# RMSNorm on one core: rows scaled on ScalarE, multiplied by gamma in bulk on VectorE, the rest in two passes on GpSimd

**Chip, cores, metric.** One core of a Trainium2 chip. The metric is device time in microseconds (us) of a whole execution, as the median of several; the profile's span is of one execution and is 1.7 to 2.5 us shorter.

## The reference

```python
x: (16, 1024, 512) float32, gamma: (512,) float32
rms = np.sqrt(np.mean(x ** 2, axis=-1, keepdims=True) + 1e-5)
return (x / rms * gamma).astype(np.float32)
```

33.6 MB are read and 33.6 MB written. The work is 4 tiles of 128 partitions x 32 rows x 512 columns, 8.39 MB each.

## The kernel before

Two kinds of on-chip memory appear below, SBUF and PSUM; in this kernel PSUM holds gamma's copy from TensorE and squares that wait to be summed. Three SBUF slots hold a tile each; tile 3 takes slot 0 after tile 0 has been stored. One row needs a sum of squares (ScalarE, for half of the groups with VectorE), a root (ScalarE), a reciprocal and one fused multiply (VectorE).

```python
load(0, 0, 0, 8); load(0, 0, 8, 32)          # SyncE's queue; (tile, slot, first row, last row)
nc.scalar.dma_start(out=gamma_row, in_=gamma.unsqueeze(0))
# ... ones x gamma_row in TensorE -> PSUM -> gamma_b [128, 512] in SBUF, copied by VectorE

def apply(slot, g, rstd):                    # 8 rows
    for r in range(G):
        nc.vector.scalar_tensor_tensor(
            out=slots[slot][:, g + r, :], in0=slots[slot][:, g + r, :],
            scalar=rstd[:, r : r + 1], in1=gamma_b, op0=OP.mult, op1=OP.mult)

def transfers(t, g):                         # after the rows of (t, g) are done
    if (t, g) == (0, 0):
        store(0, 0, 0, 1); load(1, 1, 0, 32); load(2, 2, 0, 16)
        store(0, 0, 1, 2); load(2, 2, 16, 32)
    elif (t, g) == (0, 24):
        store(0, 0, 2, 16); store(0, 0, 16, 32); load(3, 0, 0, 16); load(3, 0, 16, 32)
    elif (t, g) == (1, 24): store(1, 1, 0, 32)
    elif (t, g) == (2, 24): store(2, 2, 0, 32)
    elif (t, g) == (3, 8):  store(3, 0, 0, 16)
    elif (t, g) == (3, 24): store(3, 0, 16, 32)

ahead = row_stats(0, 0)
for k, (t, g) in enumerate(groups):          # the sums run one group ahead; a scheduler orders the rest
    ...
```

## Time and profile before

| | before |
|---|---|
| time, median (range) of 4 | 162.13 us (161.92 to 162.3) |
| span of the profiled run | 160.4 us |
| busy: VectorE, ScalarE, GpSimd | 122.6, 80.1, 0.2 us |
| share of the bulk transfer queue | 97.7% |
| tile 1, 2, 3a, 3b: store issued at | 85.6, 115.8, 131.1, 146.3 us |

The store times read as dates: in this kernel each store is issued before the queue ahead of it is empty, and the transfers run without a hole (422 to 436 GB/s from 2 to 157.6 us). The prediction shows the lines, and calls the times at which the queue would run empty the times at which it "wants" a tile. Below, "3a" and "3b" are tile 3's halves.

### The profile page before, as it was taken

Reading aid. Unit: us, or ns where it says so; the run is one execution under the profiler, and the core shown is the slowest. Engines: PE = TensorE matmul, PEld = TensorE weight load, DVE = VectorE, ACT = ScalarE, POOL = GpSimd, SP = SyncE. Lnnn points to the kernel's source line nnn. Section 1 sums busy time; section 2 is a strip of 40 time slices with the busy share of each in tenths; the row PEclk is TensorE's granted clock in tenths of the full one; section 3 lists DMA queues with packets and bytes.
Section 4 is the critical chain, followed back from the end, with each engine's and each line's share of the span. In section 5 each row is a group of like instructions: output and inputs, shape, how many; then the busy total and the mean of one; then the engine's idle time right before and its main releaser. Section 6 shows DMA issues by size and latency. Waiting matters only on the chain.

```text
span 160.4 us, 410 instructions
## 1 busy us (share of the span) xinstructions
PE 2.0 (1%) x2; PEld 0.5 (0%) x2; DVE 122.6 (76%) x163; ACT 80.1 (50%) x162; POOL 0.2 (0%) x4
## 2 busy tenths in 40 slices
PE   4000000000000000000000000000000000000000
PEld 1000000000000000000000000000000000000000
DVE  0100928999999519999999999999999999994000
ACT  3098039990390999996900950079609940000000
POOL 0000000000000000000000000000000000000000
DMA  5999999699699999999999999998998998999993
GB/s 197 523 392 392 466 449 523 261 523 523 262 402 387 455 458 418 453 415 466 409 392 498 409 400 507 409 507 376 425 507 360 441 507 360 417 400 441 449 417 147
DMA packets 2164, 67.13 MB, mean 419 GB/s; under 512 B 241, under 2 KB 241, under 8 KB 498
## 3 DMA queue, kind: packets, MB, share of 16 engines
q1 hardware_dynamic: 2160, 67.11, 97.7%
q14 instruction: 2, 0.02, 0.0%
q10 hardware_dynamic: 2, 0.00, 0.0%
HBM read 33.56 MB, written 33.55 MB: 418 GB/s over the span
## 4 chain that ended last, share of the span: by engine, by line
DVE 67%; DMA 13%; ACT 7%; issue 2%; DVEq 0%; SPq 0%
DVE slot L88 48%; DVE ss L71 18%; DMA slot<-in_x_dram 13%; ACT sq_scratch L76 3%; ACT sq L70 3%; DVE rstd L83 1%; DVEq L154 0%; ACT rms L82 0%; SPq L42 0%
## 5 line engine op out<-in xcount | busy, mean ns | idle before, releaser
L88 DVE SCALAR_TENSOR_TENSOR slot<-slot,rstd,gamma_b 128x512 f32<-128x512 f32 x128 | 85.8, 738 | 0.1
L76 ACT ACTIVATE sq_scratch<-slot 128x512 f32<-128x512 f32 x64 | 40.0, 625 | 10.0 <-DMA slot<-in_x_dram 8.7
L70 ACT ACTIVATE sq<-slot 128x2048 f32<-128x2048 f32 x16 | 29.8, 1864 | 18.6 <-DVE ss L71 11.5
L71 DVE TENSOR_REDUCE ss<-sq 128x4 f32<-128x2048 f32 x16 | 35.9, 2274 | 3.4 <-ACT sq L70 3.4
L82 ACT ACTIVATE rms<-ss,eps_t 128x8 f32<-128x8 f32 x16 | 4.6, 297 | 25.9 <-DVE ss L71 25.7
L83 DVE RECIPROCAL rstd<-rms 128x8 f32<-128x8 f32 x16 | 3.1, 193 | 16.1 <-ACT rms L82 16.1
L76 ACT ACTIVATION_READ_ACCUMULATOR sq_scratch<-slot 128x1 f32 x64 | 11.9, 186 | 0.0
L57 DVE COPY gamma_b<-sq 128x512 f32<-128x512 f32 x1 | 0.7, 691 | 3.3 <-PE sq L55 3.3
L55 PE MATMUL sq<-gamma_row,ones_col 1*128 1x512 f32 x2 | 2.0, 1122 | 2.2 <-DMA gamma_row<-in_gamma_dram 2.2
L76 ACT ACT_TABLE_LOAD x1 | 1.3, 1283 | 1.3 <-PEq L143 1.3
L82 ACT ACT_TABLE_LOAD x1 | 1.3, 1283 | 0.0
L53 DVE MEMSET ones_col<- 1x128 f32 x1 | 0.2, 165 | 0.8 <-PEq L143 0.8
L55 PEld LDWEIGHTS sq<-gamma_row,ones_col 1*128 1x128 f32 x2 | 0.5, 306 | 2.2 <-issue 2.2
L143 POOL MEMSET const-bfloat16-1.0<- 128x1 bf16 x1 | 0.1, 101 | 0.0
L143 POOL MEMSET const-uint8-127<- 128x1 uint8 x1 | 0.1, 101 | 0.0
L143 POOL MEMSET const-float32-0.0<- 128x1 f32 x1 | 0.1, 98 | 0.2 <-issue 0.2
L143 POOL MEMSET const-float32-1.0<- 128x1 f32 x1 | 0.1, 98 | 0.0
L60 DVE MEMSET eps_t<- 128x1 f32 x1 | 0.1, 59 | 0.0
## 6 DMA issues: line engine op xcount, KB each, us to landing
slot<-in_x_dram SPq DMA_DIRECT2D x4, 4096.0 KB, 27.6
out_dram<-slot SPq DMA_DIRECT2D x3, 4096.0 KB, 18.8
slot<-in_x_dram SPq DMA_DIRECT2D x1, 6144.0 KB, 21.5
out_dram<-slot SPq DMA_DIRECT2D x1, 3584.0 KB
slot<-in_x_dram SPq DMA_DIRECT2D x1, 2048.0 KB, 7.2
out_dram<-slot SPq DMA_DIRECT2D x2, 256.0 KB, 21.3
out_dram<-slot SPq DMA_DIRECT2D x2, 29.8
gamma_row<-in_gamma_dram ACTq DMA_DIRECT2D x1, 2.0 KB
```

The costliest lines, as they stand in the source:

```text
L53: nc.vector.memset(ones_col, 1.0)
L55: nc.tensor.matmul(gamma_psum[:, 0], ones_col, gamma_row, start=True, stop=True)
L57: nc.vector.tensor_copy(out=gamma_b, in_=gamma_psum[:, 0])
L60: nc.vector.memset(eps_t, eps)
L70: nc.scalar.activation(out=sq, in_=slots[slot][:, g + h : g + h + H, :], func=AF.Square)
L71: nc.vector.tensor_reduce(out=ss[:, h : h + H], in_=sq, axis=mybir.AxisListType.X, op=OP.add)
L76: nc.scalar.activation(out=sq_scratch, in_=slots[slot][:, g + r, :], func=AF.Square, accum_out=ss[:, r : r + 1],)
L82: nc.scalar.activation(out=rms, in_=ss, func=AF.Sqrt, bias=eps_t, scale=1.0 / D)
L83: nc.vector.reciprocal(out=rstd, in_=rms)
L88: nc.vector.scalar_tensor_tensor(out=slots[slot][:, g + r, :], in0=slots[slot][:, g + r, :], scalar=rstd[:, r : r + 1], in1=gamma_b, op0=O ...
L143: nc = _bacc.Bacc("TRN2", target_bir_lowering=False, num_devices=1)
```

## The change

The intent is to spread the elementwise work over three engines. ScalarE squares whole groups of rows and scales some rows by the reciprocal; VectorE sums the squares and multiplies those rows by gamma in bulk (one instruction for several rows); GpSimd takes the last rows of a group (its "share", 3 to 8 of 8 or 16) and multiplies them twice. The order on the engines is now written by hand. Cut to the core:

```diff
+    ctx.enter_context(tc.manual_schedule())
+    nc.scalar.addr_align(128, offset=0, max_nops=0)
-    nc.scalar.dma_start(out=gamma_row, in_=gamma.unsqueeze(0))
+    pieces = (0, 96, 176, 256, 336, 416, D)
+    for c0, c1 in zip(pieces, pieces[1:]):
+        nc.scalar.dma_start(out=gamma_row[:, c0:c1], in_=gamma.unsqueeze(0)[:, c0:c1])
-    nc.vector.tensor_copy(out=gamma_b, in_=gamma_psum[:, 0])
+    nc.scalar.copy(out=gamma_b[:, 0], in_=gamma_psum[:, 0])
+    groups = [    # tile, first row, rows, pieces of the squares, GpSimd's share
+        (0, 0, 8, (4, 4), 3), (0, 8, 8, (4, 4), 3), (0, 16, 16, (7, 5, 4), 7),
+        (1, 0, 16, (7, 5, 4), 8), (1, 16, 16, (7, 5, 4), 8), (2, 0, 16, (7, 5, 4), 8),
+        (2, 16, 16, (7, 5, 4), 7), (3, 0, 16, (7, 5, 4), 7), (3, 16, 16, (7, 5, 4), 3)]
+    def scale_by_pool(rstd, t, g, n, share):
+        part = slots[slot_of[t]][:, g + n - share : g + n, :]
+        by_row = rstd[:, n - share : n].to_broadcast([P, share, D])
+        nc.gpsimd.tensor_tensor(out=part, in0=part, in1=by_row, op=OP.mult)
+        last = nc.gpsimd.tensor_tensor(
+            out=part, in0=part, in1=gamma_b.to_broadcast([P, share, D]), op=OP.mult)
+    def scale_rows(rstd, t, g, r0, r1):
+        for r in range(r0, r1):
+            nc.scalar.activation(out=x[:, g + r, :], in_=x[:, g + r, :], func=AF.Copy, scale=rstd[:, r])
+        part = x[:, g + r0 : g + r1, :]
+        nc.vector.tensor_tensor(out=part, in0=part, in1=gamma_b.to_broadcast([P, r1 - r0, D]), op=OP.mult)
     # (0, 0): three single-row stores between the loads of tile 2, instead of two
# ... cut: tile 0 in three loads, load 1 issued at once; tile 2 in three loads; scheduling notes; the loop, whose order on VectorE is, per group of 16:
#     sum 7 rows, sum 5 rows, multiply (first half), sum 4 rows, multiply (second half), reciprocal
```

More of the change, by code (lines that the diff above doesn't have):

```diff
@@ L27 @@
     R = 32
-    G = 8
-    H = 4
     assert N == 4 * P * R
@@ L33 @@
     ov = of.rearrange("(t p r) d -> t p r d", p=P, r=R)
+    ctx.enter_context(tc.manual_schedule())
+    nc.scalar.addr_align(128, offset=0, max_nops=0)
     const = ctx.enter_context(tc.tile_pool(name="const", bufs=1))
-    stats = ctx.enter_context(tc.tile_pool(name="stats", bufs=4))
-    psum = ctx.enter_context(tc.tile_pool(name="psum", bufs=2, space=bass.MemoryType.PSUM))
+    stats = ctx.enter_context(tc.tile_pool(name="stats", bufs=9))
+    psum = ctx.enter_context(tc.tile_pool(name="psum", bufs=1, space=bass.MemoryType.PSUM))
@@ L39 @@
     slots = [const.tile([P, R, D], fp32, name=f"slot{i}") for i in range(3)]
+    before_scale = []
     def load(t, slot, r0, r1):
-        nc.sync.dma_start(out=slots[slot][:, r0:r1], in_=xv[t][:, r0:r1])
+        dma = nc.sync.dma_start(out=slots[slot][:, r0:r1], in_=xv[t][:, r0:r1])
+        before_scale.append((slot, r0, r1, dma))
     def store(t, slot, r0, r1):
-        nc.sync.dma_start(out=ov[t][:, r0:r1], in_=slots[slot][:, r0:r1])
+        dma = nc.sync.dma_start(out=ov[t][:, r0:r1], in_=slots[slot][:, r0:r1])
+        before_scale.append((slot, r0, r1, dma))
@@ L47 @@
     load(0, 0, 0, 8)
-    load(0, 0, 8, 32)
+    load(0, 0, 8, 16)
+    load(0, 0, 16, 32)
+    load(1, 1, 0, 32)
     gamma_row = const.tile([1, D], fp32)
-    nc.scalar.dma_start(out=gamma_row, in_=gamma.unsqueeze(0))
+    pieces = (0, 96, 176, 256, 336, 416, D)
+    for c0, c1 in zip(pieces, pieces[1:]):
+        nc.scalar.dma_start(out=gamma_row[:, c0:c1], in_=gamma.unsqueeze(0)[:, c0:c1])
     ones_col = const.tile([1, P], fp32)
-    nc.vector.memset(ones_col, 1.0)
-    gamma_psum = psum.tile([P, H, D], fp32, name="sq")
+    nc.gpsimd.memset(ones_col, 1.0)
@@ L55 @@
+    gamma_psum = psum.tile([P, 7, D], fp32, name="sq_psum")
     nc.tensor.matmul(gamma_psum[:, 0], ones_col, gamma_row, start=True, stop=True)
-    gamma_b = const.tile([P, D], fp32)
-    nc.vector.tensor_copy(out=gamma_b, in_=gamma_psum[:, 0])
+    gamma_b = const.tile([P, 1, D], fp32)
+    nc.scalar.copy(out=gamma_b[:, 0], in_=gamma_psum[:, 0])
     eps_t = const.tile([P, 1], fp32)
-    nc.vector.memset(eps_t, eps)
-    sq_scratch = const.tile([P, D], fp32)
-    def row_stats(slot, g):
-        ss = stats.tile([P, G], fp32, name="ss")
-        rms = stats.tile([P, G], fp32, name="rms")
-        rstd = stats.tile([P, G], fp32, name="rstd")
-        if (g // G) % 2:
-            for h in range(0, G, H):
-                sq = psum.tile([P, H, D], fp32, name="sq")
-                nc.scalar.activation(out=sq, in_=slots[slot][:, g + h : g + h + H, :], func=AF.Square)
-                nc.vector.tensor_reduce(
-                    out=ss[:, h : h + H], in_=sq, axis=mybir.AxisListType.X, op=OP.add
-                )
-        else:
-            for r in range(G):
-                nc.scalar.activation(
-                    out=sq_scratch,
-                    in_=slots[slot][:, g + r, :],
-                    func=AF.Square,
-                    accum_out=ss[:, r : r + 1],
-                )
-        nc.scalar.activation(out=rms, in_=ss, func=AF.Sqrt, bias=eps_t, scale=1.0 / D)
-        nc.vector.reciprocal(out=rstd, in_=rms)
-        return rstd
@@ L86, in apply @@
-    def apply(slot, g, rstd):
-        for r in range(G):
-            nc.vector.scalar_tensor_tensor(
-                out=slots[slot][:, g + r, :],
-                in0=slots[slot][:, g + r, :],
-                scalar=rstd[:, r : r + 1],
-                in1=gamma_b,
-                op0=OP.mult,
-                op1=OP.mult,
-            )
-    groups = [(t, g) for t in range(4) for g in range(0, R, G)]
-    slot_of = [0, 1, 2, 0]
+    nc.gpsimd.memset(eps_t, eps)
+    groups = [
+        (0, 0, 8, (4, 4), 3),
+        (0, 8, 8, (4, 4), 3),
+        (0, 16, 16, (7, 5, 4), 7),
+        (1, 0, 16, (7, 5, 4), 8),
+        (1, 16, 16, (7, 5, 4), 8),
+        (2, 0, 16, (7, 5, 4), 8),
+        (2, 16, 16, (7, 5, 4), 7),
+        (3, 0, 16, (7, 5, 4), 7),
+        (3, 16, 16, (7, 5, 4), 3),
+    ]
@@ new lines, with square_sums, inverse_rms @@
+    slot_of = [0, 1, 2, 0]
+    def square_sums(ss, t, g, r, m, k):
+        home, name, most = ((psum, "sq_psum", 7), (const, "sq_sbuf", 5))[k % 2]
+        sq = home.tile([P, most, D], fp32, name=name)
+        rows = slots[slot_of[t]][:, g + r : g + r + m, :]
+        nc.scalar.activation(out=sq[:, :m], in_=rows, func=AF.Square)
+        nc.vector.tensor_reduce(
+            out=ss[:, r : r + m, 0], in_=sq[:, :m], axis=mybir.AxisListType.X, op=OP.add
+        )
+    def inverse_rms(ss, n):
+        nc.scalar.activation(out=ss[:, :n, 0], in_=ss[:, :n, 0], func=AF.Sqrt, bias=eps_t, scale=1.0 / D)
+        nc.vector.reciprocal(out=ss[:, :n, 0], in_=ss[:, :n, 0])
+        return ss
@@ new lines, in scale_by_pool @@
+    def scale_by_pool(rstd, t, g, n, share):
[3 more added lines that the diff above has]
+        last = nc.gpsimd.tensor_tensor(
+            out=part, in0=part, in1=gamma_b.to_broadcast([P, share, D]), op=OP.mult
+        )
+        before_scale.append((slot_of[t], g + n - share, g + n, last))
+    def scale_rows(rstd, t, g, r0, r1):
+        x = slots[slot_of[t]]
+        for r in range(r0, r1):
+            nc.scalar.activation(out=x[:, g + r, :], in_=x[:, g + r, :], func=AF.Copy, scale=rstd[:, r])
+        part = x[:, g + r0 : g + r1, :]
+        scaled = nc.vector.tensor_tensor(out=part, in0=part, in1=gamma_b.to_broadcast([P, r1 - r0, D]), op=OP.mult)
+        for slot, b0, b1, earlier in before_scale:
+            if slot == slot_of[t] and b0 < g + r1 and g + r0 < b1:
+                tc.declare_no_dep(scaled.ins, earlier.ins, reason="ScalarE waited for it before it scaled these rows")
@@ L102, in transfers @@
             store(0, 0, 0, 1)
-            load(1, 1, 0, 32)
             load(2, 2, 0, 16)
             store(0, 0, 1, 2)
-            load(2, 2, 16, 32)
-        elif (t, g) == (0, 24):
-            store(0, 0, 2, 16)
+            load(2, 2, 16, 24)
+            store(0, 0, 2, 3)
+            load(2, 2, 24, 32)
+        elif (t, g) == (0, 16):
+            store(0, 0, 3, 16)
             store(0, 0, 16, 32)
@@ L111, in transfers, with pieces_of @@
             load(3, 0, 16, 32)
-        elif (t, g) == (1, 24):
+        elif (t, g) == (1, 16):
             store(1, 1, 0, 32)
-        elif (t, g) == (2, 24):
+        elif (t, g) == (2, 16):
             store(2, 2, 0, 32)
-        elif (t, g) == (3, 8):
+        elif (t, g) == (3, 0):
             store(3, 0, 0, 16)
-        elif (t, g) == (3, 24):
+        elif (t, g) == (3, 16):
             store(3, 0, 16, 32)
-    ahead = row_stats(0, 0)
-    for k, (t, g) in enumerate(groups):
-        rstd = ahead
-        if k + 1 < len(groups):
-            tn, gn = groups[k + 1]
-            ahead = row_stats(slot_of[tn], gn)
-        apply(slot_of[t], g, rstd)
+    def pieces_of(group):
+        t, g, n, pieces, share = group
+        ss = stats.tile([P, 16, 1], fp32, name="ss")
+        r = 0
+        todo = []
+        for k, m in enumerate(pieces):
+            todo.append((ss, t, g, r, m, k))
+            r += m
+        return ss, todo
+    ss, todo = pieces_of(groups[0])
+    for piece in todo:
+        square_sums(*piece)
+    rstd = inverse_rms(ss, groups[0][2])
+    for k, group in enumerate(groups):
+        t, g, n, pieces, share = group
+        mine = n - share
+        half = (mine + 1) // 2
+        ahead = groups[k + 1 :][:1]
+        ss, todo = pieces_of(ahead[0]) if ahead else (None, [])
+        scale_by_pool(rstd, t, g, n, share)
+        for piece in todo[:2]:
+            square_sums(*piece)
+        if n < 16:
+            scale_rows(rstd, t, g, 0, mine)
+        else:
+            scale_rows(rstd, t, g, 0, half)
+        for piece in todo[2:]:
+            square_sums(*piece)
+        if n == 16:
+            scale_rows(rstd, t, g, half, mine)
         transfers(t, g)
+        for nxt in ahead:
+            rstd = inverse_rms(ss, nxt[2])
 _INS = ['x', 'gamma']
```

## The prediction

It is printed as recorded, less passages that are cut and marked. The reason given against the transfer-bound rival and the one given for the lock were of that kind too. Its sums came to: VectorE about 112 us in all; tile 1 ready at 96 us, tile 2 at 130, tile 3's halves at 146 and 152.5, and so the central case of 174 us; under the lock in full 22.6 us a group with 8 GpSimd rows and 20.9 with 7, and so 195 to 201 us. "Port" and "lock" are words for a supposition that no trace had shown. The rival's 1.8 ns a column is an estimate: 58.5 us, from tile 1's first reciprocal near 60 us to 118.5 us, for 31 rows of 512 columns, twice.

> **What bounds the kernel now.** I read the page's slices and queue shares first, then the rates in stretches of the span, then the order of the stores, then the groups.
>
> ```profile
> span 160.4 us, 410 instructions
> ...
> PE 2.0 (1%) x2; PEld 0.5 (0%) x2; DVE 122.6 (76%) x163; ACT 80.1 (50%) x162; POOL 0.2 (0%) x4
> ...
> DMA  5999999699699999999999999998998998999993
> ...
> q1 hardware_dynamic: 2160, 67.11, 97.7%
> ```
>
> No compute engine is full; the queue of bulk transfers is, at 97.7% of the span. The rate in stretches (last two columns: DMA share, GB/s):
>
> ```profile
> 2.00:20.00 18.00, 2.04 (x2) 0.50 (x2) 5.03 (x9) 7.92 (x19) 0.00 (x0) 1.00 0.99 422
> 20.00:60.00 40.00, 0.00 (x0) 0.00 (x0) 31.19 (x37) 26.88 (x46) 0.00 (x0) 1.00 1.00 424
> 60.00:100.00 40.00, 0.00 (x0) 0.00 (x0) 40.00 (x58) 24.92 (x57) 0.00 (x0) 1.00 1.01 436
> 100.00:140.00 40.00, 0.00 (x0) 0.00 (x0) 39.96 (x52) 19.63 (x41) 0.00 (x0) 1.00 1.00 432
> 140.00:157.60 17.60, 0.00 (x0) 0.00 (x0) 6.23 (x10) 0.00 (x0) 0.00 (x0) 1.00 1.00 434
> 157.60:160.40 2.80, 0.00 (x0) 0.00 (x0) 0.00 (x0) 0.00 (x0) 0.00 (x0) 1.00 0.06 23
> ```
>
> From 2 to 157.6 us the transfers run at 422 to 436 GB/s with no hole. The page's chain of work that ended last is 67% VectorE, but that chain only leads back from the last store's issue; what counts is whether a store is issued before the queue in front of it runs dry. SyncE's issues answer that:
>
> ```profile
> 36.95 13.21 SPq L45 DMA_DIRECT2D out_dram<-slot  x2
> 72.22 10.13 SPq L42 DMA_DIRECT2D slot<-in_x_dram  x2
> ...
> 115.83 30.76 SPq L45 DMA_DIRECT2D out_dram<-slot  x3
> ```
>
> At 0.432 MB/us a half tile (16 rows, 4.19 MB) takes 9.7 us, a whole tile 19.4. Stream order: loads 0, 1, 2 with a few rows stored (from 1.7 to about 62 us), rest of tile 0 out (to 80), tile 3 in (to 99), tile 1 out (to 118.5), tile 2 out (to 138), tile 3 out (to 157.5). So the queue wants tile 1 by 99, tile 2 by 118.5, tile 3's halves by 138 and 148. The kernel before issues these at 85.6, 115.8, 131.1 and 146.3 us: margins of 13, 3, 7 and 1.5 us. It's at the transfers' floor, and computing faster buys nothing: without startup and tail the bytes need about 155.5 of the 160.4 us.
>
> ```profile
> L88 DVE SCALAR_TENSOR_TENSOR slot<-slot,rstd,gamma_b 128x512 f32<-128x512 f32 x128 | 85.8, 738 | 0.1
> L70 ACT ACTIVATE sq<-slot 128x2048 f32<-128x2048 f32 x16 | 29.8, 1864 | 18.6 <-DVE ss L71 11.5
> L71 DVE TENSOR_REDUCE ss<-sq 128x4 f32<-128x2048 f32 x16 | 35.9, 2274 | 3.4 <-ACT sq L70 3.4
> ```
>
> These give the unit prices for the new work: squares of 4 rows 1.86 us on ScalarE, their sum 2.27 us (2.2 from start to start) on VectorE.
>
> [...]
>
> **The change part by part.** The bytes are the same, and so is the stream order in all that matters. Splits of loads, a third single-row store (0.26 MB) and gamma in six pieces only shift issues; at 0.51 us an issue on ScalarE, gamma's six end near 4 us, before tile 0's first data (7.98 us). I give them 0 ± 0.5 us. The chains in engine order:
>
> - VectorE loses 85.8 us of row multiplies. It sums the squares of all 128 rows per partition (twice the 35.9 us for 64 rows, less some fixed cost: about 69) and multiplies 74 rows by gamma in bulk[...]. With reciprocals about 112 us, only 11 below 122.6.
> - ScalarE squares all rows in large pieces (about 58 us) and scales 74 rows at an estimated 0.61 us (the 512-column form is 0.625 in the trace with an accumulator): 45. With roots about 106, up from 80.
> - GpSimd gets the other 54 rows (shares 3, 3, 7, 8, 8, 8, 7, 7, 3), twice[...], and cannot start before the first reciprocals.
>
> Per 16-row group: ScalarE 7.2 + 8.5 x 0.61 + 0.3 = 12.7; VectorE 8.9 + 4.6 + 0.2 = 13.7, or about 14.5 with its wait for the first squares[...]. The transfers want a group every 19.4 us of load and store, which looks like enough, but not from where GpSimd starts.
>
> Tile 1 lands near 42 (ScalarE was released by it at 42.74 before). Its first squares (7 rows, 3.1) end near 46; VectorE then sums 3.85 and 2.75, multiplies 2.7, sums 2.2, multiplies 2.2, takes the reciprocal 0.2: near 60. From there GpSimd is back to back[...]. Store 2 starts near 131.4 after issue and first-byte time, a hole of about 13 us. After that 16.8 MB remain: 131.4 + 38.8 = 170.2, and both halves of tile 3 are ready in time (wanted by 150.8 and 160.5). Plus 2.4 us tail gives a span of 172.6; the time is 1.8 above the span before, so about 174 us. That is my central case: the last but one store waits for GpSimd.
>
> **The rivals.**
> - Still bound by transfers. If GpSimd's pass costs at most about 1.8 ns a column and the port isn't taken for whole instructions, tile 2 is ready by about 119 and the hole goes: 161 to 163 us. For it: the shares look fitted to the engine (few rows at both ends, 7 or 8 between), and ScalarE and VectorE alone meet every date.[...]
> - The port lock in full. A 16-row group then runs pass, multiply, pass, multiply in turn[...]. From 62 us (the reciprocal also waits for the lock): tile 1 at 108, tile 2 at 152, holes of about 9 and 24 us plus a few at the end: about 195 to 201 us.[...] Against: a kernel fitted on a chip would not have ended up with this. If blocking is partial, 175 to 190.
> - A gain. The mean rate from 2 to 157.6 us is 430 GB/s and the best stretch 436: running all of it at 436 would save 155.6 x (1 - 430/436) = 2.1 us, 1.3%. Over 2% would need 3.2 us; startup and tail are unchanged.
>
> **Range and chances.** I give the transfer-bound rival 0.36, GpSimd alone 0.25, blocking in part or in full 0.37, a gain 0.02. The number on record is the central case, 174, which also has about half of the weight on either side; the low end must hold the transfer-bound case (161), the high end most of the lock (200). The distribution has two humps, so the number between is the least bad and the range is wide.
>
> **What would show it.** Right: GpSimd[...] back to back from near 60 us; the DMA line falls below 9 around 118 to 131; SyncE's wait for GpSimd ends the wait before tile 2's store. Lock: bulk multiplies on VectorE of 4 to 5 rows showing far over their 2.2 to 2.8 us, or idle time before them with the passes next to them stretched, and holes before tiles 1 and 2. Transfer-bound: the DMA line stays at 9 to the end and store 2 is issued by 118. Wrong in kind: a hole before load 2 or load 3[...].

Some of its prices stand there without a source; the runs give them. VectorE's multiplies by gamma, put at 2.2 us for 4 rows, 2.7 for 5 and 4.6 for a group with 8 GpSimd rows, take 2.28, 2.81 and 2 x 2.28 = 4.56 us in run 1. A sum takes 2.28 us for 2048 columns and 3.89 for 3584 there, so 1.05 ns a column and some 0.13 us fixed. From readiness to a store's first bytes the prediction allows 1.4 us; the first bytes follow the start of an issue by 1.0 us in the kernel before (0.73 to 1.7 us) and by 0.8 us at tile 1's store in the changed one (112.49 to 113.3).

## The result, and the profile after

The changed kernel takes 205.94 us (205.41 to 209.05, 4 runs, one of them slow) against 162.13: a ratio of 1.2692, 95% interval 1.2644 to 1.274. Ratios here are the mean time of one kernel's runs over that of the other's of the same rounds, so not quite the ratio of the medians. That is outside the predicted range, which ended at 200. Executions over 1.5% slower than the fastest of the same kernel are left out of the means. The page of the changed kernel:

```profile
span 203.2 us, 288 instructions
...
PE 2.0 (1%) x2; PEld 0.5 (0%) x2; DVE 156.8 (77%) x50; ACT 108.2 (53%) x111; POOL 108.2 (53%) x24
...
DMA  7999999989999999999500999900004999499297
```

VectorE was to fall to about 112 us and shows 156.8. The transfers, full before, now stand still twice. In stretches (GB/s last):

```profile
2.00:99.00 97.00, 2.04 (x2) 0.49 (x2) 72.14 (x27) 60.83 (x58) 51.09 (x10) 1.00 1.00 429
99.00:113.00 14.00, 0.00 (x0) 0.00 (x0) 13.58 (x4) 3.62 (x4) 7.21 (x2) 1.00 0.02 7
113.00:132.00 19.00, 0.00 (x0) 0.00 (x0) 18.36 (x4) 9.57 (x11) 15.49 (x2) 1.00 1.02 442
132.00:157.00 25.00, 0.00 (x0) 0.00 (x0) 23.54 (x9) 15.66 (x15) 14.23 (x3) 1.00 0.00 0
```

The rate between the holes is no lower than before. The two long holes end where SyncE issues tile 1's store (112.49 us, before 85.63) and tile 2's (156.50, before 115.83); with one of some 2 us before 3a's store (177.8) and one of some 4 us before the last (191.3) they are about 45 us, and the span grew by 42.8. What SyncE waits for last before the stores of tiles 1 and 2 is a VectorE multiply: the one that ends at 112.4 us releases tile 1, whose GpSimd rows were done at 105.9. So the question is what makes tiles 1 and 2 late. One group of 16 rows on VectorE, in order of time:

```profile
66.94 0.24 DVE L96 RECIPROCAL ss<-ss 128x16 f32<-128x16 f32 x1
68.24 3.89 DVE L90 TENSOR_REDUCE ss<-sq_psum 128x7 f32<-128x3584 f32 x1 [1.06 <-ACT sq_psum L89]
72.05 2.81 DVE L90 TENSOR_REDUCE ss<-sq_sbuf 128x5 f32<-128x2560 f32 x1
74.78 10.54 DVE L113 TENSOR_TENSOR slot<-slot,gamma_b 128x2048 f32<-128x2048 f32 x1
85.24 2.28 DVE L90 TENSOR_REDUCE ss<-sq_psum 128x4 f32<-128x2048 f32 x1
87.44 2.27 DVE L113 TENSOR_TENSOR slot<-slot,gamma_b 128x2048 f32<-128x2048 f32 x1
89.64 0.24 DVE L96 RECIPROCAL ss<-ss 128x16 f32<-128x16 f32 x1
```

and the same stretch on GpSimd:

```profile
67.26 7.02 POOL L102 TENSOR_TENSOR slot<-slot,ss 128x4096 f32<-128x4096 f32 x1 [7.32 <-DVE ss L96]
74.36 8.81 POOL L103 TENSOR_TENSOR slot<-slot,gamma_b 128x4096 f32<-128x4096 f32 x1
89.96 7.02 POOL L102 TENSOR_TENSOR slot<-slot,ss 128x4096 f32<-128x4096 f32 x1 [6.79 <-DVE ss L96]
```

There are two multiplies of the same shape in the group: one takes 2.27 us, the other 10.54. The slow one starts 0.42 us after GpSimd's second pass and ends at 85.32, which is 2.15 us after that pass ends (74.36 + 8.81 = 83.17): the wait, then the work. It's shown as busy, not as idle. Behind it, in order, stand VectorE's next sum, then the root on ScalarE, then the reciprocal, and GpSimd's next group waits for that reciprocal (6.8 us idle). So the period is a closed chain (times from start to start, since neighbours in the trace overlap by some 0.1 us): passes 7.0 + 8.8, multiply 2.2, sum 2.2, multiply 2.2, reciprocal and gaps 0.3 = 22.7 us. VectorE's sum of 5 rows, which reads a single SBUF tile, ran beside the first pass in 2.81 us, the mean of all seven of its kind (the third line of VectorE's view). Summed over the kernel, the profile's line of this multiply holds 85.5 us in the changed kernel and 41.8 where nothing blocks it (first experiment below).

A second thing is new at the start:

```profile
12.98 2.04 PE L64 MATMUL sq_psum<-gamma_row,ones_col 1*128 1x512 f32 x2 [12.98 <-DMA gamma_row<-in_gamma_dram]
...
15.68 1.88 ACT L89 ACTIVATE sq_psum<-slot 128x2048 f32<-128x2048 f32 x1
```

Gamma lands at 13.0 us (2.2 before), and since ScalarE copies it ahead of its first square, that square starts at 15.68 instead of 7.98 us, although tile 0's first rows are there (in run 11, with the same loads, they let the first square start at 8.06).

### The profile page after: what moved, and what is told of

The parts are those of the page before. It is cut to its first block, busy times and chain, and to the rows that moved or that the text cites. A ratio compares the mean times of both kernels' runs of the same rounds, so it can differ in the third digit from the quotient of the medians.

```text
span 203.2 us, 288 instructions
## 1 busy us (share of the span) xinstructions
PE 2.0 (1%) x2; PEld 0.5 (0%) x2; DVE 156.8 (77%) x50; ACT 108.2 (53%) x111; POOL 108.2 (53%) x24
## 4 chain that ended last, share of the span: by engine, by line
DVE 66%; ACT 18%; DMA 4%; ACTq 2%; DVEq 2%; PE 1%; issue 1%
DVE slot L113 33%; DVE ss L90 33%; ACT sq_psum L89 12%; DMA gamma_row<-in_gamma_dram 4%; ACT slot L111 3%; ACTq L60 2%; DVEq L199 2%; PE sq_psum L64 1%; ACT sq_sbuf L89 1%; ACT ss L95 1%; ACT L95 1%; ACTq L199 0%; ACT gamma_b L66 0%; DVE ss L96 0%; ACTq L34 0%
## 5 line engine op out<-in xcount | busy, mean ns | idle before, releaser
L113 DVE TENSOR_TENSOR slot<-slot,gamma_b 128x2048 f32<-128x2048 f32 (+3 forms) x16 | 85.5, 5352 | 4.9 <-ACT slot L111 4.9
L102 POOL TENSOR_TENSOR slot<-slot,ss 128x1536 f32<-128x1536 f32 (+2 forms) x9 | 47.8, 5308 | 74.8 <-DVE ss L96 74.8
L90 DVE TENSOR_REDUCE ss<-sq_psum 128x4 f32<-128x2048 f32 (+1 forms) x16 | 47.8, 2985 | 27.5 <-ACT sq_psum L89 27.5
L103 POOL TENSOR_TENSOR slot<-slot,gamma_b 128x1536 f32<-128x1536 f32 (+2 forms) x9 | 60.0, 6667 | 0.7
L111 ACT ACTIVATE slot<-slot,ss 128x512 f32<-128x512 f32 x74 | 46.7, 707 | 2.1 <-DVE ss L96 2.1
L89 ACT ACTIVATE sq_psum<-slot 128x2048 f32<-128x2048 f32 (+1 forms) x16 | 38.7, 2421 | 0.0
L95 ACT ACTIVATE ss<-ss,eps_t 128x16 f32<-128x16 f32 (+1 forms) x9 | 2.7, 304 | 59.1 <-DVE ss L90 59.1
L90 DVE TENSOR_REDUCE ss<-sq_sbuf 128x5 f32<-128x2560 f32 (+1 forms) x9 | 24.2, 2689 | 0.0
L89 ACT ACTIVATE sq_sbuf<-slot 128x2560 f32<-128x2560 f32 (+1 forms) x9 | 20.0, 2226 | 0.0
L96 DVE RECIPROCAL ss<-ss 128x16 f32<-128x16 f32 (+1 forms) x9 | 2.1, 232 | 2.1 <-ACT ss L95 2.1
## 6 DMA issues: line engine op xcount, KB each, us to landing
slot<-in_x_dram SPq DMA_DIRECT2D x4, 2048.0 KB, 11.8
```

Of the source, the lines that this page charges most:

```text
L89: nc.scalar.activation(out=sq[:, :m], in_=rows, func=AF.Square)
L90: nc.vector.tensor_reduce(out=ss[:, r : r + m, 0], in_=sq[:, :m], axis=mybir.AxisListType.X, op=OP.add)
L95: nc.scalar.activation(out=ss[:, :n, 0], in_=ss[:, :n, 0], func=AF.Sqrt, bias=eps_t, scale=1.0 / D)
L96: nc.vector.reciprocal(out=ss[:, :n, 0], in_=ss[:, :n, 0])
L102: nc.gpsimd.tensor_tensor(out=part, in0=part, in1=by_row, op=OP.mult)
L103: last = nc.gpsimd.tensor_tensor(out=part, in0=part, in1=gamma_b.to_broadcast([P, share, D]), op=OP.mult)
```

## The experiments

Theory: a VectorE multiply with two SBUF inputs waits for a whole GpSimd pass. "Port" in the expectations is the prediction's word for what the two engines would then share; the runs show who waits for whom, not a port. Rivals: the hand-written order is too serial in itself; the bulk form with a broadcast operand is slow; the engines lack capacity; the early stores or loads hold something up. All eleven runs gave correct results; each is beside 7 runs of the kernel before on the same chip (162.17 to 162.39 us).

**1. Gamma from PSUM for VectorE.** One operand's memory changes (gamma gets a PSUM tile of its own, since the squares reuse the old one), nothing else in schedule or shares.

```diff
-    gamma_psum = psum.tile([P, 7, D], fp32, name="sq_psum")
+    gamma_psum = psum.tile([P, 1, D], fp32, name="gamma_psum")
-        scaled = nc.vector.tensor_tensor(out=part, in0=part, in1=gamma_b.to_broadcast(...), op=OP.mult)
+        scaled = nc.vector.tensor_tensor(out=part, in0=part, in1=gamma_psum.to_broadcast(...), op=OP.mult)
```

> Edit: VectorE's bulk multiply reads gamma from a PSUM bank, so it has one SBUF input; schedule, shares and GpSimd's work stay. Theory (a VectorE multiply with two SBUF inputs waits for GpSimd's whole passes): the first multiply of a group, 9.1 to 10.6 us in the changed kernel, falls to 2.2 to 2.8 us, GpSimd runs back to back (15.9 us a group of 8 rows), tile 2's store is issued near 125 us instead of 156.5, and the time falls from 206 to 166-170 us. Rival 1 (the new fixed order is too serial, ScalarE waits for VectorE whatever the port does): the group period stays above 20 us and the time above 195. Rival 2 (the broadcast gamma operand itself makes the bulk form slow): multiplies stay over 5 us.

Measured: 167.96 us (167.37 to 168.46), ratio 1.0355. VectorE's busy time falls from 156.8 to 112.9 us with the same 50 instructions. The multiply now runs beside a pass:

```profile
62.53 7.02 POOL L102 TENSOR_TENSOR slot<-slot,ss 128x4096 f32<-128x4096 f32 x1 [2.67 <-DVE ss L96]
69.62 8.87 POOL L103 TENSOR_TENSOR slot<-slot,gamma_b 128x4096 f32<-128x4096 f32 x1
70.05 2.28 DVE L113 TENSOR_TENSOR slot<-slot,gamma_psum 128x2048 f32<-128x2048 f32 x1
```

It starts 0.43 us into the pass, as in the changed kernel, and takes 2.28 us. GpSimd's passes are as long as before (7.02 and 8.87), so it had lost nothing by the blocking itself; it lost by waiting for the reciprocals. Tile 2's store comes at 124.3 us. Order, broadcast form and capacity are the same as in the changed kernel, so those rivals can't explain more than the 5.8 us that remain.

**2. GpSimd's share cut to 4 rows** in the six middle groups.

```diff
-        (1, 0, 16, (7, 5, 4), 8),     # and likewise the five others with 7 or 8
+        (1, 0, 16, (7, 5, 4), 4),
```

> Edit: GpSimd's share is 4 rows in every 16-row group but the last (which keeps 3), everything else as changed. Theory (port): both passes together take about 8 us and are over about when VectorE's first multiply is ready, 7.7 us after the reciprocal, so it waits at most about 0.5 us; VectorE then sets a period of about 16.7 us (8.9 sums, 6.4 multiplies, 1.2 rest) and the time is 171-178 us, although VectorE and ScalarE do more. Rival (the two engines are short of capacity, and GpSimd's help is what keeps it at 206): giving work back to VectorE makes it slower than 206.

Measured: 178.29 us, ratio 1.0979, just over the top of the expected range. The multiply met the second pass's last 1.8 us (4.96 us shown instead of 3.35), where I had allowed 0.5. Less help from GpSimd makes the kernel 27.7 us faster: capacity was not the shortage.

**3. Gamma in one transfer.**

```diff
-    pieces = (0, 96, 176, 256, 336, 416, D)
+    pieces = (0, D)
```

> Edit: gamma is loaded by one transfer of 512 columns instead of six. In the changed kernel the last piece lands near 13.0 us (2.2 before) and ScalarE's first square waits for the gamma copy in front of it until 15.7 us (8.0 before). If the six pieces are the reason: the first square starts at 8 to 9 us, the reciprocal of group 3 comes about 6 to 7 us earlier (60 instead of 67), and the time falls by 5 to 8 us to 198-201. If it is ScalarE's later first issue (1.16 instead of 0.72 us, behind the loads), the one transfer lands late too and the time stays within 2 us of 206. The port's stalls (9 to 10.6 us multiplies) stay in either case.

Measured: 201.28 us, ratio 1.2409: 4.7 us less, just short of the expected gain. Gamma lands at 7.9 us, between the two cases of the expectation, and the first square starts at 10.58. The pieces are part of the delay; run 11 takes up the rest.

**4. GpSimd's passes cut into single rows.**

```diff
-        nc.gpsimd.tensor_tensor(out=part, in0=part, in1=by_row, op=OP.mult)
+        for r in range(n - share, n):        # and the same for the gamma pass
+            part = slots[slot_of[t]][:, g + r : g + r + 1, :]
+            nc.gpsimd.tensor_tensor(out=part, in0=part, in1=rstd[:, r : r + 1].to_broadcast([P, 1, D]), op=OP.mult)
```

> Edit: each GpSimd pass is cut into instructions of one row (512 columns), same bytes and order. If the port is held for one GpSimd instruction at a time: VectorE's first multiply waits at most one row's piece, about 1.2 us, so it shows 2.2 to 4 us instead of 9 to 10.6, GpSimd's passes stretch by VectorE's 2.2 us each, and the period falls from 22.7 to about 20-21.5 us: 188-202 us. If instead GpSimd keeps the port from piece to piece as long as more work is queued, or if the two simply share bandwidth, the multiply stays at 9 us or over and the time at 206 or above.

Measured: 206.61 us, ratio 1.2761. The time is the expectation's second case, the instructions behave as in its first. VectorE's multiplies of 2048 columns average 2.55 us (5.03 before the cut). What happened shows in one pair:

```profile
70.25 3.04 DVE L113 TENSOR_TENSOR slot<-slot,gamma_b 128x2048 f32<-128x2048 f32 x1
...
71.10 3.08 POOL L102 TENSOR_TENSOR slot<-slot,ss 128x512 f32<-128x512 f32 x1
```

VectorE waits 0.8 us for the end of one row's instruction, then GpSimd's next row waits for VectorE's multiply: 3.08 us for an instruction that takes 1.04 alone. The blocking is mutual, from instruction to instruction. What I missed is the price of cutting: a row costs 1.04 and 1.26 us where its share of the long passes was 0.88 and 1.10, so GpSimd's own work is 8 x (1.0 + 1.25) = 18 us a group (start to start). VectorE now runs ahead (about 15 us a group), so some three of its multiplies fall into each GpSimd group, which takes 23.9 us (66.12 to 90.05). GpSimd has become the slowest part, SyncE waits for it, and tile 2's store comes later than in the changed kernel (163.35 against 156.50 us); in return no hole is left after that store. These effects cancel, and the equal time alone would have led to the wrong conclusion.

**5. Both single edits, 1 and 3.**

```diff
-    pieces = (0, 96, 176, 256, 336, 416, D)
+    pieces = (0, D)
-    ... in1=gamma_b.to_broadcast(...)      # VectorE's multiply
+    ... in1=gamma_psum.to_broadcast(...)
```

> Edit: both single edits together, gamma in one transfer and read from PSUM by VectorE's multiplies. GpSimd's back-to-back passes are then the bound. With gamma alone in one piece the first square came 5.1 us earlier, but group 3 also waits for tile 1's data (near 43 us), so its reciprocal moves only about 2 us (62.2 to 60) and the time falls by 1.5 to 3 us from 168.0: 165-166.5 us. Rival: if the two gains added up in full (205.9 - 38 - 4.7) it would be 163.3 or less.

Measured: 165.1 us, ratio 1.017. The two gains don't add: taking gamma in one transfer saves 4.7 us with the blocking and 2.9 without it. GpSimd's passes stand back to back from 60 to 142 us, and tile 2's store comes at 121.7 us.

**6. As 5, with a share of 7 in place of 8** in groups (1,0), (1,16) and (2,0).

```diff
-        (1, 0, 16, (7, 5, 4), 8),     # and likewise the two others
+        (1, 0, 16, (7, 5, 4), 7),
```

> Edit: as the run before it, and GpSimd's share is 7 rows instead of 8 in three groups. GpSimd's chain loses 3 x 2 us, so tile 2 is ready near 118, when the transfer queue wants it, VectorE's group takes about 15 us and fits: the time is 161.5-163.5 us, the same as the kernel before within 1%. If something other than GpSimd's passes holds tile 2 back, it stays at 165 or above.

Measured: 164.38 us (162.72 to 164.8), ratio 1.0103 (1.004 to 1.0166): about 1% slower than the kernel before, and 0.9 us over what I expected. GpSimd now waits 0.94 us for VectorE in each group, whose period is 15.0 us (one more row in its multiplies than in run 5, 1.06 us of wait for the first squares). Tile 2's store comes at 119.8 us, only 1.9 us earlier. The bound had passed from GpSimd to VectorE.

**7. The kernel before, with 12 GpSimd multiplies that nobody waits for.**

```diff
+    pad = const.tile([P, 4, D], fp32)
+    nc.gpsimd.memset(pad, 1.0)
+    for _ in range(12):
+        nc.gpsimd.tensor_tensor(out=pad, in0=pad, in1=pad, op=OP.mult)
```

> Edit: the kernel before, with 12 GpSimd multiplies of 2048 columns on a tile of their own (reads SBUF, result unused), which no other engine waits for and which waits for none. Theory (port, instruction by instruction): while they run, each row multiply of VectorE (two SBUF inputs) that meets one waits for its end, up to about 4.4 us; 10 or so of the 128 show it, the group's busy time rises from 85.8 to 110-135 us, and the time rises by 5 to 45 us. Rival (GpSimd work costs others nothing unless they wait for its result): row multiplies stay at 738 ns, time 162.

Measured: 181.05 us, ratio 1.1155. The instructions' order on VectorE, ScalarE and SyncE is that of the kernel before; only the side work is new. The pad is a tile of its own, so the collision doesn't need an operand that both engines read, as gamma_b is in the changed kernel. The two engines take turns, one instruction each:

```profile
17.33 3.93 POOL L66 TENSOR_TENSOR pad<-pad 128x2048 f32<-128x2048 f32 x1
17.72 4.08 DVE L93 SCALAR_TENSOR_TENSOR slot<-slot,rstd,gamma_b 128x512 f32<-128x512 f32 x1
21.33 3.93 POOL L66 TENSOR_TENSOR pad<-pad 128x2048 f32<-128x2048 f32 x1
21.72 4.08 DVE L93 SCALAR_TENSOR_TENSOR slot<-slot,rstd,gamma_b 128x512 f32<-128x512 f32 x1
```

A row multiply of 0.66 us (start to start) comes through once in 4.01 us; eight of them take 30.1 us instead of 5.4. A pass takes 3.93 us, 3.60 where no multiply meets it. The busy time of VectorE's row multiplies rises from 85.8 to 110.6 us, and tile 1's store moves from 85.6 to 106.7.

**8. The kernel before, with 60 GpSimd fills.**

```diff
+    pad = const.tile([P, 4, D], fp32)
+    for _ in range(60):
+        nc.gpsimd.memset(pad, 1.0)
```

> Edit: the kernel before, with 60 GpSimd fills of 2048 columns (writes SBUF only, reads nothing), for tens of us beside VectorE's row multiplies. If only GpSimd's reads take the port[...]: row multiplies stay at 738 ns and the time at 162 within 1%. If any GpSimd work takes it: row multiplies lengthen to 1-2 us while the fills run and their busy time rises by 20 us or more.

Measured: 161.95 us, ratio 0.9978:

```profile
L65 POOL MEMSET pad<- 128x2048 f32 x60 | 108.3, 1806 | 3.7 <-POOLq L147 0.3
L92 DVE SCALAR_TENSOR_TENSOR slot<-slot,rstd,gamma_b 128x512 f32<-128x512 f32 x128 | 85.9, 742 | 0.1
```

108 us of GpSimd work that only writes cost nothing. In the runs here only GpSimd work that reads SBUF collides. A GpSimd instruction with a single SBUF input was not tried.

**9. Without the three early single-row stores.**

```diff
-            store(0, 0, 0, 1)     # likewise rows 1 and 2
...
-            store(0, 0, 3, 16)
+            store(0, 0, 0, 16)
```

> Edit: the changed kernel without the three early single-row stores; rows 0 to 15 of tile 0 leave in one store. Tile 1's and tile 2's stores wait for the chain of VectorE and GpSimd, which this does not touch, so the time stays at 206 within 1.5 us. Rival: the early stores pace the loads of tile 2; without them load 2 is issued near 9 us instead of 34, something before 100 us in the transfer queue moves, and the time changes by more than 2 us either way.

Measured: 206.66 us, ratio 1.2709; the changed kernel 1.2692. All loads of tile 2 are issued by 11.8 us and nothing follows from it.

**10. Each group's GpSimd rows in two halves.**

```diff
+        cut = n - share // 2
+        for r0, r1 in ((n - share, cut), (cut, n)):      # both passes for each half
```

> Edit: the changed kernel with each group's GpSimd rows cut in two halves, each with its two passes, so four instructions of about 3.5 and 4.4 us instead of two of 7.0 and 8.8. The port's own sum for a group of 8 rows is 7.0 + 8.8 + 2.2 + 2.2 = 20.2 us. If the port is handed over at each instruction's end and idles in the changed kernel for the rest of the 22.7 us period, the period falls to 20.5-21.5, VectorE's first multiply shows 3 to 7 us, tile 2's store comes near 149-153 us, and the time is 198-203 us. If it stays at 206, the period is not set by the port's idle time.

Measured: 195.34 us, ratio 1.2015, faster than expected; the hole before the last store went too (issued at 177.06; from 171.5 to 190 us the rate is 425 GB/s). Multiplies of 2048 columns average 3.64 us, a group takes 20.3 us (65.16 to 85.47 us on GpSimd), and tile 2's store comes at 149.5 us. Of the 22.7 us period in the changed kernel the two engines' turns fill 7.0 + 8.8 + 2.2 + 2.2 = 20.2; the 20.3 here is close to that, so what went was the idle rest.

**11. Gamma in one transfer, without the alignment instruction ahead of it.**

```diff
-    nc.scalar.addr_align(128, offset=0, max_nops=0)
-    pieces = (0, 96, 176, 256, 336, 416, D)
+    pieces = (0, D)
```

> Edit: gamma in one transfer, and the instruction that aligns ScalarE's program (0.4 us ahead of its first issue) taken out, so that gamma is issued at about 0.72 us, with the first load instead of after it. If gamma was late because it was issued behind the loads, it lands near 2.2 us (7.9 with the one transfer alone), the first square starts at 8 us with tile 0's data, VectorE's first multiply of tile 0's last group is no longer held, and the time falls 1.5 to 3 us below the 201.3 us of the one transfer alone. If it still lands near 8 us, the place of the issue is not the reason, and the time stays within 1 us of 201.3.

Measured: 198.11 us, ratio 1.2197: 3.2 us below run 3, 7.8 below the changed kernel.

```profile
0.73 0.51 ACTq L59 DMA_DIRECT2D gamma_row<-in_gamma_dram  x1
...
2.17 2.04 PE L63 MATMUL sq_psum<-gamma_row,ones_col 1*128 1x512 f32 x2 [2.17 <-DMA gamma_row<-in_gamma_dram]
...
8.06 1.88 ACT L88 ACTIVATE sq_psum<-slot 128x2048 f32<-128x2048 f32 x1 [3.23 <-DMA slot<-in_x_dram]
```

In run 3 the same 2 KB, issued from 1.18 us on, took 2.67 us to issue and landed at 7.9. 0.45 us in the place of the issue went with 5.7 us in landing. What inside the issue or the queue does this was not separated.

Most of the 7.8 us is the blocking again. This is the first multiply of tile 0's last group, in the changed kernel and in run 11:

```profile
55.18 7.44 DVE L113 TENSOR_TENSOR slot<-slot,gamma_b 128x2560 f32<-128x2560 f32 x1
...
52.17 2.85 DVE L112 TENSOR_TENSOR slot<-slot,gamma_b 128x2560 f32<-128x2560 f32 x1
```

It starts 3.0 us later in the changed kernel, about what run 5 shows for an earlier gamma where nothing blocks (2.9 us). But there it starts 3.0 us into a pass (52.17 to 59.93), where in run 11 the pass ends 0.16 us after it starts, and so it ends 7.6 us later.

| run | edit | time, us | ratio to before |
|---|---|---|---|
| changed kernel | | 205.94 | 1.2692 |
| 1 | gamma from PSUM | 167.96 | 1.0355 |
| 2 | share 4 | 178.29 | 1.0979 |
| 3 | gamma in one transfer | 201.28 | 1.2409 |
| 4 | passes row by row | 206.61 | 1.2761 |
| 5 | 1 and 3 | 165.1 | 1.017 |
| 6 | 5, share 7 | 164.38 | 1.0103 |
| 7 | before, with GpSimd reads | 181.05 | 1.1155 |
| 8 | before, with GpSimd fills | 161.95 | 0.9978 |
| 9 | no early row stores | 206.66 | 1.2709 |
| 10 | passes in halves | 195.34 | 1.2015 |
| 11 | gamma in one transfer, early | 198.11 | 1.2197 |

No version is faster than the kernel before by more than the 0.2% of run 8, which only adds fills to it. The kernel before runs its transfers without a hole, so a better division of the compute has nothing to win there; the best repaired version of the changed one (run 6) stays about 1% behind it, with an interval of 0.4 to 1.7%.

## Why the prediction was wrong

- **The bound before** was read rightly: transfers, with dates for the stores. The dates held: the queue ran empty at 99 us before tile 1's store, as worked out.
- **VectorE's and ScalarE's work** was priced rightly: about 112 and 106 us predicted; 112.9 and 108.2 measured where nothing blocks.
- **GpSimd's price** was a little high. It was one figure for both passes, shown by no trace or run here. Measured: 108.2 us in all; the pass by the reciprocal costs 1.71 ns a column (7.02 us for 4096), the pass by gamma 2.15 (8.81 us). The shorter passes of run 2 differ likewise (3.60 and 4.52 us for 2048 columns).
- **The step that failed: "From there GpSimd is back to back".** The central case of 174 us took GpSimd's passes as running free of VectorE. Run 1 is that case on the chip: passes back to back, tile 2's store waiting for GpSimd. It gave 168.0, lower than 174 because a group of 8 rows cost GpSimd 15.9 us, less than at the price. So the arithmetic was sound up to that price, and the premise was wrong. In the changed kernel GpSimd waits 6.8 to 7.3 us in each group with 8 GpSimd rows for a reciprocal that stands, in VectorE's order, behind a multiply that waits for GpSimd.
- **The right mechanism was on the page of rivals, underrated.** The lock in full was worked out at 22.6 us a group and "about 195 to 201 us"; the period measured is 22.7. That the two agree is luck: the passes took 7.0 + 8.8 us, less than at the price, and the chain left out a sum of 2.2 us that stands behind the blocked multiply. The order inside was different too: the first multiply misses the gap between the passes by 0.42 us and waits for the second. What was right is the mechanism, that a multiply waits for a whole pass (10.54 us for one of 2.27). It got 0.37 together with partial blocking, because "a kernel fitted on a chip would not have ended up with this". That is an argument about an author, not about a machine, and nothing in the trace supported it.
- **The term that carried it past the range: gamma, "0 ± 0.5 us".** I worked out when the six issues end (near 4 us; measured 5.1) and not when the last piece lands (13.0 us), nor that its copy now stands ahead of ScalarE's first square. The term measures 2.9 us where nothing blocks (run 5 against run 1, with gamma at 8.0 instead of 13.0 us) and 7.8 us with the blocking (run 11 against the changed kernel). With gamma on time run 11 takes 198.1 us, inside the 195 to 201 of the lock rival and inside the range.
- **The single-row stores** were rightly given nothing (run 9: 206.66 against 205.94).

## What to carry to other kernels

Before moving elementwise work to GpSimd, list the VectorE instructions with two SBUF inputs that will run beside it: in the runs here each of them could wait for a whole GpSimd instruction that reads SBUF, and everything behind it in order waited too; one operand in PSUM took that away here (206 to 168 us). A blocked VectorE instruction looks busy in the profile (10.54 us for a multiply of 2.27), so compare the durations of equal shapes, not the busy share. And when a small transfer moves behind large ones in issue order, look for who waits for its landing, not only for when it is issued (2 KB landed at 7.9 us in run 3, at 2.2 in run 11, issued 0.45 us earlier).
